# A feed-forward whose first product is made of seven block products instead of eight, on one Trainium2 core

## The chip, the cores and the metric

The kernel runs on one core of one Trainium2 chip. The metric is the device time of one execution in microseconds; three runs of the kernel before are shown, and their median counts.

## What is computed

One layer of a sequence encoder on 512 tokens of width 2048, all in float32. Four mixers (HGRN2, S5, stick-breaking attention, RWKV-7) give `mix`; the part that the change touches is what follows:

```python
mod = c_act @ ada_w[l] + ada_b[l]
shift1, scale1, gate1, shift2, scale2, gate2 = [m[:, None, :] for m in jnp.split(mod, 6, axis=-1)]
...
mix = jnp.concatenate([o_a, o_b, o_c, o_d], axis=-1) @ w_out[l]
x = _layer_norm(DEEPNORM_ALPHA * x + gate1 * mix, ln1_g[l], ln1_b[l])

h = x * (1.0 + scale2) + shift2
ffn = (jax.nn.silu(h @ ffn_w1[l]) * (h @ ffn_w3[l])) @ ffn_w2[l]
x = _layer_norm(DEEPNORM_ALPHA * x + gate2 * ffn, ln2_g[l], ln2_b[l])
```

`ffn_w1` and `ffn_w3` are 2048 x 5632, `ffn_w2` is 5632 x 2048.

## The kernel before

**Products.** Every large product is made in three passes: each operand is split into a high part (ACT rounds it to fp32r) and a low part (DVE subtracts the high part from the value), and `mm3` (L586) multiplies high by high, low by high and high by low, three matmuls into the same PSUM bank. A matmul has a stationary block of 128 x 128 and 512 moving columns. `wload` (L574) brings 256 KB of weights by a DMA on SP's queue into `wr`, casts them to `wh` on ACT and makes `wl` on DVE, with three buffers of each.

**Order.** A scheduler puts the instructions of each engine into one fixed order, by priorities: `tc.high_priority` in `wload` moves a load and its split ahead. Each engine then works through its row, and waits where an operand isn't there yet. Pools of rotating tiles decide how far ahead a load may go: a tile is free again when its last reader is done. PSUM has eight banks, four in the pool `pd` and four in `pm`.

**End of the first half.** `w_out` (L1414) makes the mixers' output product in groups of feature tiles; per column block n four PSUM sums are multiplied by the gate `g1` into `go` and added to `acc` by DVE (`add_out`, L1409). The steps W1, B1 and W2 are the last in `ORDER`. The group 8 to 11 comes after them: its weights are multiplied by the gate beforehand (`wr`), split into `woh` and `wol`, the features into `cath` and `catl`, and the sums go straight into `acc`, t by t, each t with its `layer_norm` (L1195) and a scaling.

**Feed-forward.** 64 transposes on PE turn `acc` into 16 feature tiles (`hf`, then `hh`, `hl`), 128 features x 512 tokens. `ff_pair(f)` (L1503) makes 128 hidden columns: 16 `mm3` for `ffn_w1` into `pu`, 16 for `ffn_w3` into `pv`, with the weights stationary and the features moving; then silu, a product, and a split into `gh`, `gl`. After each eight f (the last time four) comes the second product over them: for four column blocks of 512, four PSUM sums over eight f, gated and added into `acc`. The last group of four has gated weights made beforehand, so that only an addition, a layer norm and eight scalings per t stand behind the last matmuls. The gate `gate2` (part 5 of the modulation) comes from 64 loads `aw` and 64 DVE steps `acc<-aw,cact,acc` that `pump` (L1148) puts between the steps of W1, W2 and `ff_pair`.

Of the kernel before, what the change touches and what calls it, by code (L numbers as in the profile page):

```python
# [573 lines left out]
def wload(E, src, r0, c0, kk, cols):  # L574

    with E.tc.high_priority(offset=E.ahead):
        raw = E.wp.tile([128, kk, cols], F32, name=E.nm("wr"), tag="wr")
        E.nc.sync.dma_start(out=raw, in_=src[r0 : r0 + 128 * kk, c0 : c0 + cols].rearrange("(k p) c -> p k c", p=128))
# [7 lines left out]
def mm3(E, out, a, b, first, last):  # L586

    E.mm(out, a[0], b[0], first, False)
    E.mm(out, a[1], b[0], False, False)
    E.mm(out, a[0], b[1], False, last)  # L590

# [624 lines left out]
def body(ctx, tc, i, out):  # L1216
# [263 lines left out]
    E.h = []  # L1480
    for k in range(KT):
# [5 lines left out]
        hi, lo = E.sb("hh", dt=F32R, pool=E.hp), E.sb("hl", dt=F32R, pool=E.hp)  # L1487
        nc.vector.tensor_copy(out=hi, in_=f)
        E.sub(lo, f, hi.bitcast(F32))
        E.h.append((hi, lo))  # L1490
    ada_queue(E, [(5, b) for b in range(4)])
    E.rate = 1

    for n in range(4):
        w = slice(T * n, T * n + T)
        g, b = bcast(E, i["ln1_g"][0:1, w], "lg"), bcast(E, i["ln1_b"][0:1, w], "lb")
        E.ts(g, g, ALPHA, ALU.mult)
        E.ts(b, b, ALPHA, ALU.mult)
        for t in range(4):
            E.mul(acc[t][n], acc[t][n], g)  # L1500
            E.add(acc[t][n], acc[t][n], b)

    def ff_pair(f):  # L1503
        pu = E.psd()
        for kg in range(4):
            wh, wl = wload(E, i["ffn_w1"][0], T * kg, 128 * f, 4, 128)
            for k in range(4):
                kk = 4 * kg + k
                mm3(E, pu, (wh[:, k], wl[:, k]), E.h[kk], kk == 0, kk == 15)
        pv = E.psd()  # L1510
        for kg in range(4):
            wh, wl = wload(E, i["ffn_w3"][0], T * kg, 128 * f, 4, 128)
            for k in range(4):
                kk = 4 * kg + k
                mm3(E, pv, (wh[:, k], wl[:, k]), E.h[kk], kk == 0, kk == 15)
            pump(E, 5)
        s = E.sb("s")
        E.act(s, pu, AF.Silu)
        E.mul(s, s, pv)
        hi = E.sb("gh", dt=F32R, pool=E.pp)  # L1520
        lo = E.sb("gl", dt=F32R)
        E.copy(hi, s)
        E.sub(lo, s, hi.bitcast(F32))
# [2 lines left out]
    f = 0
    for cnt in (8, 8, 8, 8, 8, 4):
        fs = list(range(f, f + cnt))
        f += cnt
        ws = []  # L1530

        def gated(n, k):
            if k == fs[0]:
                ws.append(bcast(E, E.gate[5][0:1, T * n : T * n + T], "g2", E.ap))
            r = E.sb("wr", pool=E.pp)
            nc.sync.dma_start(out=r, in_=i["ffn_w2"][0, 128 * k : 128 * k + 128, T * n : T * n + T])
            E.mul(r, r, ws[n])
            return r

        if cnt < 8:  # L1540
            raw = {(n, k): gated(n, k) for n in range(3) for k in fs}
        gs = [ff_pair(a) for a in fs]
        if cnt == 8:
            for n in range(4):
                g2 = bcast(E, E.gate[5][0:1, T * n : T * n + T], "g2")
                pss = [E.psm() for _ in range(4)]
                for kk, k in enumerate(fs):
                    wh, wl = wload(E, i["ffn_w2"][0], 128 * k, T * n, 1, T)
                    for t in range(4):
                        w = slice(128 * t, 128 * t + 128)  # L1550
                        mm3(E, pss[t], (gs[kk][0][:, w], gs[kk][1][:, w]), (wh[:, 0], wl[:, 0]), kk == 0, kk == 7)
                for t in range(4):
                    add_out(pss[t], g2, acc[t][n])
        else:
            raw.update({(3, k): gated(3, k) for k in fs})
            ws = {a: E.split(r, "w2", E.hp) for a, r in raw.items()}
            lg = [bcast(E, i["ln2_g"][0:1, T * n : T * n + T], "lg") for n in range(4)]
            lb = [bcast(E, i["ln2_b"][0:1, T * n : T * n + T], "lb") for n in range(4)]
            for t in range(4):
                w = slice(128 * t, 128 * t + 128)  # L1560
                for n in range(4):
                    ps = E.psm()
                    for kk, k in enumerate(fs):
                        mm3(E, ps, (gs[kk][0][:, w], gs[kk][1][:, w]), ws[n, k], kk == 0, kk == cnt - 1)
                    E.add(acc[t][n], acc[t][n], ps)
                mu, rs = layer_norm(E, acc[t])
                for n in range(4):
                    E.stt(acc[t][n], acc[t][n], mu, lg[n], ALU.subtract, ALU.mult)
                    E.stt(acc[t][n], acc[t][n], rs, lb[n], ALU.mult, ALU.add)
                    nc.sync.dma_start(out=out[0, w, T * n : T * n + T], in_=acc[t][n])  # L1570


# [24 lines left out]
```

## Time and profile before

| | us |
|---|---|
| runs | 2560.27, 2562.38, 2572.34 |
| median | 2562.38 |
| profiled execution | 2564.39 |
| its span | 2562.7 |
| granted TensorE clock, mean over the span | 0.992 |

The profile shows one execution. PE is TensorE's matmuls, PEld its weight loads, DVE VectorE, ACT ScalarE, POOL GpSimd, SP the engine that issues most DMAs. A group of instructions is told as line, engine, operation, output and inputs by the program's names, shape and count; then busy time, mean duration in ns of one, and the idle time of the engine ahead of them with what ended it. The duration of a matmul is longer than the distance from one to the next, since they overlap; so what a matmul costs is read from counts over a stretch. The chain that ended last follows the work back from the last instruction.

The stages that matter here, by their times in the profiled execution: the last group of w_out from 1048 us to 1092, the feed-forward from 1099 to 2548, of which the first product is 4224 matmuls and the second 2112, and the end of the last layer norm to 2562.7.

### The profile page before, as it was taken

The numbers are of one execution on the slowest core, as the hardware profiler recorded it, in microseconds if no ns is written. First come the engines' busy times: TensorE is split into PE (matmuls) and PEld (weight loads), VectorE is DVE, ScalarE is ACT, GpSimd is POOL, SyncE is SP. The second block draws the span as 40 slices with busy tenths as digits, with TensorE's granted clock in tenths as the row PEclk, the third lists the DMA queues.
The fourth block names the chain that finished last, engine by engine and source line by source line (L and its number), as shares of the span: only waits on it lengthen the run. The fifth ranks groups of instructions, "written<-read, shape, count | busy, mean of one in ns | idle before, by whom it ended". The sixth has DMA issues, their size and how long they took to land.

```text
span 2562.7 us, 33154 instructions
## 1 busy us (share of the span) xinstructions
PE 2506.0 (98%) x12242; PEld 1966.0 (77%) x12242; DVE 1419.9 (55%) x2562; ACT 801.3 (31%) x1409; POOL 71.5 (3%) x193
## 2 busy tenths in 40 slices
PE   8999999999999989999999999999999999999997
PEld 3557767776788767877888888888888888888886
DVE  3755997466788978895344334433443334334538
ACT  2435242322544643132222222222222222222231
POOL 3300000110000000000000000000000000000000
PEclk9999999999999999999999999999999999999999
DMA  9876235445744676135333333333333333334333
GB/s 296 263 245 189 78 88 141 116 122 157 222 117 127 191 231 209 58 91 181 101 110 99 98 98 108 100 98 97 109 100 98 98 104 105 97 98 141 122 95 109
DMA packets 405874, 340.00 MB, mean 133 GB/s; under 512 B 38374, under 2 KB 325312, under 8 KB 405712
## 3 DMA queue, kind: packets, MB, share of 16 engines
q1 hardware_dynamic: 402976, 337.16, 43.2%
q8 instruction: 96, 1.57, 0.3%
q10 hardware_dynamic: 2256, 0.67, 0.1%
q14 instruction: 66, 0.54, 0.1%
q0 software_dynamic: 480, 0.05, 0.0%
HBM read 330.96 MB, written 6.83 MB: 132 GB/s over the span
## 4 chain that ended last, share of the span: by engine, by line
PE 85%; DVE 7%; DMA 5%; issue 1%; ACT 1%; SPq 0%; DVEq 0%; POOL 0%
PE pd L87 55%; PE pm L87 29%; DMA aw<-in_ada_w_dram 5%; DVE acc L117 2%; DVE wl L99 1%; PE pm L90 1%; DMA wr<-in_w_out_dram 0%; DVE acc L99 0%; DVE st L1200 0%; DVE sl L120 0%; DVE wr L99 0%; SPq L1086 0%; DVE sz L99 0%; ACT wh L96 0%; DVE sl L117 0%
## 5 line engine op out<-in xcount | busy, mean ns | idle before, releaser
L99 DVE TENSOR_TENSOR wl<-wr,wh 128x512 fp32r<-128x512 f32 x748 | 516.5, 692 | 844.3 <-ACT wh L96 791.2
L96 ACT CAST wh<-wr 128x512 fp32r<-128x512 f32 x748 | 463.8, 620 | 1356.2 <-PE pd L87 929.7
L87 PE MATMUL pd<-hh,wl 128*128 128x512 f32 x1920 | 754.6, 393 | 3.6 <-DVE wl L99 3.5
L87 PE MATMUL pd<-hh,wh 128*128 128x512 f32 x1920 | 754.7, 393 | 2.4 <-ACT hh L96 2.4
L87 PE MATMUL pd<-hl,wh 128*128 128x512 f32 x1920 | 753.5, 393 | 0.0
L87 PEld LDWEIGHTS pd<-hh,wh 128*128 128x128 f32 x1920 | 361.6, 188 | 92.2 <-ACT wh L96 8.0
L87 PEld LDWEIGHTS pd<-hh,wl 128*128 128x128 f32 x1920 | 361.6, 188 | 89.9 <-issue 8.7
L87 PEld LDWEIGHTS pd<-hl,wh 128*128 128x128 f32 x1920 | 361.6, 188 | 78.6 <-issue 4.0
L87 PE MATMUL pm<-wl,gh 128*128 128x512 f32 x640 | 249.2, 389 | 0.0
L87 PE MATMUL pm<-wh,gl 128*128 128x512 f32 x640 | 249.1, 389 | 0.0
L87 PE MATMUL pm<-wh,gh 128*128 128x512 f32 x640 | 248.2, 392 | 0.0
L117 DVE SCALAR_TENSOR_TENSOR acc<-aw,cact,acc 128x512 f32<-128x512 f32 x240 | 179.9, 749 | 65.1 <-DMA aw<-in_ada_w_dram 63.2
L87 PEld LDWEIGHTS pm<-wh,gh 128*128 128x128 f32 x640 | 120.1, 188 | 28.6 <-DVE go L99 3.8
L87 PEld LDWEIGHTS pm<-wl,gh 128*128 128x128 f32 x640 | 120.1, 188 | 25.2
L87 PEld LDWEIGHTS pm<-wh,gl 128*128 128x128 f32 x640 | 120.2, 188 | 24.3
L87 PE MATMUL pd<-wh,cath 128*128 128x512 f32 x192 | 76.6, 403 | 7.0 <-DVE go L99 7.0
L87 PE MATMUL pd<-wl,cath 128*128 128x512 f32 x192 | 76.0, 398 | 1.4 <-DVE wl L99 1.4
L87 PE MATMUL pd<-wh,catl 128*128 128x512 f32 x192 | 76.3, 397 | 0.0
L87 PE MATMUL pm<-aw,crep 128*32 128x512 f32 x256 | 71.3, 614 | 4.9 <-DVE hgm L233 4.3
L99 DVE TENSOR_TENSOR acc<-acc,go 128x512 f32<-128x512 f32 x112 | 72.3, 687 | 0.0
L99 DVE TENSOR_TENSOR s<-s,pd 128x512 f32<-128x512 f32 x44 | 30.3, 688 | 55.7 <-PE pd L87 55.7
L99 DVE TENSOR_TENSOR go<-pm,g 128x512 f32<-128x512 f32 x80 | 51.3, 684 | 0.0
(449 smaller groups left out, 2415.5 us busy)
## 6 DMA issues: line engine op xcount, KB each, us to landing
wr<-in_ffn_w_dram SPq DMA_DIRECT2D x528, 256.0 KB, 2.9
aw<-in_ada_w_dram SPq DMA_DIRECT2D x384, 256.0 KB, 3.5
wr<-in_w_in_dram SPq DMA_DIRECT2D x184, 256.0 KB, 3.0
wr<-in_w_out_dram SPq DMA_DIRECT2D x64, 256.0 KB, 3.5
g<-gate SPq DMA_DIRECT2D x36, 256.0 KB, 3.7
x<-in_x_dram SPq DMA_DIRECT2D x16, 256.0 KB, 5.0
acc<-in_x_dram SPq DMA_DIRECT2D x16, 256.0 KB, 5.0
out_dram<-acc SPq DMA_DIRECT2D x16, 256.0 KB, 2.1
```

The costliest lines, as they stand in the source:

```text
L87: return self.nc.tensor.matmul(out=out, lhsT=lhsT, rhs=rhs, start=start, stop=stop, **kw)
L90: self.nc.tensor.transpose(out=out, in_=in_, identity=self.ident)
L96: self.nc.scalar.copy(out=out, in_=in_)
L99: self.nc.vector.tensor_tensor(out=out, in0=a, in1=b, op=op)
L117: self.nc.vector.scalar_tensor_tensor(out=out, in0=a, scalar=s, in1=b, op0=op0, op1=op1)
```

## The change

**First product.** The features and the two weight matrices are seen as blocks. A pair (j, j+8) of feature tiles, each halved into 256 tokens, gives four blocks of the left operand; `ffn_w1` and `ffn_w3`, rows j and j+8, 512 columns, give four blocks of the right one, which is the products' moving operand now. Sums of blocks (Winograd's form of Strassen's scheme) need seven block products where eight were made. Sums of features are made once, before the feed-forward; sums of weights for every j of every block of 512 columns. A block of columns n (eleven of them) has two stages: stage 1 makes p1, p3, p2 over j = 0 to 7 from three quarter-blocks of weights that are only split; stage 2 makes the rest of p1 and p4, p7, p5 from four quarter-blocks, with three sums on DVE (`wx`) and two splits. Then u, v, g1, g2 are put together from the PSUM sums on ACT and DVE, and `turned` transposes the result on PE, splits it and stores it to a DRAM tile `gd`.

**Second product.** It runs after all columns of the first, in two halves r of 1024 output columns; 22 pairs of f each, sums staying in eight PSUM banks over all 44 f. The gated features are read back from `gd`. The sums of `gate2` are made in the first half, four loads and steps in each of 16 pairs. `acc`, normalised, is stored to DRAM (`xn`) ahead of the feed-forward and read back in the second half. The last pair is done t by t, each t followed by gate, sum, layer norm, eight scalings and the stores.

**Pools.** The pools of the first half are opened in stacks that are closed before the feed-forward, and the pools of the weights (`wp`, `ap`, `a1`) already before the last group of w_out, whose gate broadcasts now take tiles of the pool `tp`.

The diff, cut to what the prediction speaks of:

```diff
+    E.high.close()
+    late = ExitStack()
+    E.ax = E.open(late, "ax", 8, side="right")
     grp = (8, 9, 10, 11)
     ws = {}
     for n in range(4):
-        g1 = bcast(E, E.gate[2][0:1, T * n : T * n + T], "g1", E.ap)
+        g1 = bcast(E, E.gate[2][0:1, T * n : T * n + T], "g1")
...
+    for j in range(8):
+        f, e = feature(j), feature(j + 8)
+        a11, a21, a12, a22 = f[:, 0:H], f[:, H:], e[:, 0:H], e[:, H:]
+        s, r = E.sb("hs"), E.sb("hr")
+        s1, s2, s3, s4 = r[:, 0:H], r[:, H:], s[:, 0:H], s[:, H:]
+        E.add(s1, a21, a22)
+        E.sub(s2, s1, a11)
+        E.sub(s4, a12, s2)
+        E.sub(s3, a11, a21)
+        m = {}
+        one = slot("ha")
+        E.copy(one[:, 0:H], a11)
+        E.sub(one[:, H:], a11, one[:, 0:H].bitcast(F32))
+        m["11"] = one[:, 0:H], one[:, H:]
+        m["12"], m["22"] = halves(e, "hb")
+        m["s3"], m["s4"] = halves(s, "hc")
+        m["s1"], m["s2"] = halves(r, "hd")
+        A.append(m)
...
+    E.fx = E.open(ffn_w, "fx", 2)
+    E.fh = E.open(ffn_w, "fh", 4)
+    E.ft = E.open(ffn_t, "ft", 1)
+    E.f2 = E.open(ffn_t, "f2", 2)
+    E.p2 = E.open(last, "p2", 4, space=PSUM)
...
+    def product(p, a, w, c, first, last, **kw):
+        for b in range(2):
+            v = slice(128 * b, 128 * b + 128)
+            mm3(E, p[:, b], (a[0][:, v], a[1][:, v]), (w[0][:, c], w[1][:, c]), first, last, **kw)
...
+        p1, p2, p3 = bank2("p1"), bank2("p2"), bank2("p3")
+        for j in range(8):
+            with tc.high_priority(offset=E.ahead):
+                x = quad(j, n, (0, 2, 3))
+                wa = parts(x[:, 2:4])
+                hi, lo = two(E.fh, "wh", "wh", F32R), two(E.fh, "wl", "wl", F32R)
+                E.copy(hi[:, 0], x[:, 0])
+                E.sub(lo[:, 0], x[:, 0], hi[:, 0].bitcast(F32))
+            product(p1, A[j]["11"], (hi, lo), 0, j == 0, j == 7)
+            product(p3, A[j]["s4"], wa, 0, j == 0, j == 7)
+            product(p2, A[j]["12"], wa, 1, j == 0, j == 7)
+            if before and j == 3:
+                turned(*before)
+        with soon():
+            u, v, g1 = two(E.ft, "u", "u"), two(E.ft, "v", "v"), two(E.f2, "g1", "g1")
+            E.copy(u, p1)
+            E.copy(v, p3)
+            E.add(g1, u, p2)
+            E.act(g1, g1, AF.Silu)
...
+            with tc.high_priority(offset=E.ahead):
+                x = quad(j, n, (0, 1, 2, 3))
+                E.sub(x[:, 0:2], x[:, 1:3], x[:, 0:2])
+                E.sub(x[:, 2], x[:, 2], x[:, 0])
+                E.sub(x[:, 3], x[:, 2], x[:, 3])
+                wb = parts(x[:, 2:4])
+                wa = parts(x[:, 0:2])
+            product(p1, A[j]["s2"], wb, 0, False, j == 7, skip_group_check=True)
+            product(p4, A[j]["22"], wb, 1, j == 0, j == 7)
+            product(p7, A[j]["s3"], wa, 1, j == 0, j == 7)
+            product(p5, A[j]["s1"], wa, 0, j == 0, j == 7)
+        with soon():
+            u = two(E.ft, "u", "u")
+            E.copy(u, p1)
+            E.add(v, v, p1)
+            E.add(u, u, p7)
+            g2 = two(E.ft, "g2", "g2")
+            E.sub(g2, u, p4)
+            E.act(g2, g2, AF.Silu)
+            E.add(v, v, p5)
+            E.add(u, u, p5)
+            E.mul(g1, g1, v)
+            E.mul(g2, g2, u)
+        before = n, (g1, g2)
...
+                                for n in range(2):
+                                    o = E.sb("go", pool=E.fz)
+                                    E.mul(o, pt[t][:, n], g2[2 + n])
+                                    E.add(acc[t][2 + n], acc[t][2 + n], o)
+                                mu, rs = layer_norm(E, acc[t])
```

`parts` casts 1024 columns on ACT (`wh`) and subtracts on DVE (`wl`); `quad` issues one DMA of 256 KB for each quarter-block into `wx`. A `product` is six matmuls of 128x512 into a tile of two banks; `p2` has four such tiles. `halves` splits a 512-column pair of blocks in the same way. Stage 1 has 18 matmuls per j, stage 2 has 24.

How the change moves instructions, in the order of each engine. On DVE, where w_out's last group begins, the row before (`go_2061` and `go_2062` are the last evacuation of W2, `wol` a low part of the gated weights, `acc<-acc,pd` the group's first sums; the weights' gate products `wr<-wr,g1` stand more than 180 rows earlier):

```order
L99 TENSOR_TENSOR acc_1922_8940<-acc_1922_8940,go_2061_9539 128x512
L99 TENSOR_TENSOR acc_1923_8943<-acc_1923_8943,go_2062_9542 128x512
L99 TENSOR_TENSOR wl_2240_10278<-wr_2238_10275,wh_2239_10277 128x512
L99 TENSOR_TENSOR wol_2111_9655<-wr_2109_9651,woh_2110_9654 128x512
L99 TENSOR_TENSOR acc_1809_8412<-acc_1809_8412,pd_2123_9681 128x512
L99 TENSOR_TENSOR wol_2114_9662<-wr_2112_9658,woh_2113_9661 128x512
L99 TENSOR_TENSOR acc_1846_8586<-acc_1846_8586,pd_2124_9695 128x512
```

At the same place in the changed kernel:

```order
L104 TENSOR_TENSOR acc_1922_8940<-acc_1922_8940,go_2061_9539 128x512
L104 TENSOR_TENSOR acc_1923_8943<-acc_1923_8943,go_2062_9542 128x512
L104 TENSOR_TENSOR wr_2064_9553<-wr_2064_9553,g1_2063_9551 128x512
L104 TENSOR_TENSOR wr_2067_9560<-wr_2067_9560,g1_2063_9551 128x512
L104 TENSOR_TENSOR wr_2070_9567<-wr_2070_9567,g1_2063_9551 128x512
L104 TENSOR_TENSOR wol_2066_9557<-wr_2064_9553,woh_2065_9556 128x512
L104 TENSOR_TENSOR wr_2073_9574<-wr_2073_9574,g1_2063_9551 128x512
L104 TENSOR_TENSOR wol_2069_9564<-wr_2067_9560,woh_2068_9563 128x512
```

All 16 gate products, 16 low parts of weights and four of features now stand between W2's last evacuation and the first sum `acc<-acc,pd`, 36 rows in all.

On PE, at the beginning of the feed-forward (`pm<-ident,acc` is a transpose, `hh` and `hl` are features, `wh` and `wl` weights), before:

```order
L90 MATMUL pm_2179_10061<-ident_94,acc_1849_8595 128x128
L87 MATMUL pd_2231_10238<-hh_2161_10013,wh_2233_10241 128x512
L90 MATMUL pm_2183_10072<-ident_94,acc_1846_8586 128x128
L90 MATMUL pm_2183_10072<-ident_94,acc_1847_8589 128x128
L90 MATMUL pm_2183_10072<-ident_94,acc_1848_8592 128x128
L90 MATMUL pm_2183_10072<-ident_94,acc_1849_8595 128x128
L87 MATMUL pd_2231_10238<-hh_2161_10013,wl_2234_10242 128x512
```

In the changed kernel all 64 transposes stand ahead of the first matmul of the feed-forward:

```order
L95 MATMUL pm_2252_10265<-ident_94,acc_1922_8940 128x128
L95 MATMUL pm_2252_10265<-ident_94,acc_1923_8943 128x128
L92 MATMUL p1_2263_10330<-wh_2269_10341,ha_2165_10033 128x512 x2
L92 MATMUL p3_2265_10332<-wh_2267_10337,hch_2168_10040 128x512
L92 MATMUL p1_2263_10330<-wl_2270_10342,ha_2165_10033 128x512
```

The low part `wl_2270` that its third row reads stands in DVE's row behind the last low part of the features' sums, and so do all low parts of weights.

On DVE in the first product, before (`acc<-aw,cact,acc` is a step of the modulation, `s<-s,pd` the product behind the silu):

```order
L99 TENSOR_TENSOR wl_2427_11071<-wr_2425_11068,wh_2426_11070 128x512
L117 SCALAR_TENSOR_TENSOR acc_2366_10814<-aw_2406_10988,cact_88,acc_2366_10814 128x512
L99 TENSOR_TENSOR wl_2430_11089<-wr_2428_11086,wh_2429_11088 128x512
L117 SCALAR_TENSOR_TENSOR acc_2366_10814<-aw_2407_10991,cact_88,acc_2366_10814 128x512
L117 SCALAR_TENSOR_TENSOR acc_2366_10814<-aw_2408_10994,cact_88,acc_2366_10814 128x512
L99 TENSOR_TENSOR s_2421_11060<-s_2421_11060,pd_2401_10966 128x512
```

In the changed kernel, at the beginning of stage 2 of the second block of columns (`wx` are the sums of weights of j = 0, 1, 2, `g1<-u,p2` the sum that waits for stage 1's last matmul):

```order
L104 TENSOR_TENSOR wx_2409_11197<-wx_2409_11197 128x1024
L104 TENSOR_TENSOR wx_2409_11197<-wx_2409_11197 128x512 x2
L104 TENSOR_TENSOR wx_2414_11237<-wx_2414_11237 128x1024
L104 TENSOR_TENSOR g1_2405_11189<-u_2403_11187,p2_2355_10915 128x1024
L104 TENSOR_TENSOR wl_2411_11206<-wx_2409_11197,wh_2410_11205 128x1024
L104 TENSOR_TENSOR wl_2413_11210<-wx_2409_11197,wh_2412_11209 128x1024
L104 TENSOR_TENSOR wx_2414_11237<-wx_2414_11237 128x512 x2
L104 TENSOR_TENSOR wl_2416_11246<-wx_2414_11237,wh_2415_11245 128x1024
L104 TENSOR_TENSOR wl_2418_11250<-wx_2414_11237,wh_2417_11249 128x1024
L104 TENSOR_TENSOR wx_2419_11277<-wx_2419_11277 128x1024
L104 TENSOR_TENSOR wx_2419_11277<-wx_2419_11277 128x512 x2
```

A low part 512 columns wide, one for each 256 KB, has become three sums and two low parts of 1024 columns for each 1 MB, one j after the other.

More of the change, by code (lines that the diff above doesn't have):

```diff
@@ L583, in wload, with mm3 @@
     return hi, lo
[L586 to L590, printed above, removed]
+def mm3(E, out, a, b, first, last, **kw):
+    E.mm(out, a[0], b[0], first, False, **kw)
+    E.mm(out, a[1], b[0], False, False, **kw)
+    E.mm(out, a[0], b[1], False, last, **kw)
 def rw_setup(E):
@@ L1479, in body, with slot, halves, feature @@
     E.add(sh, sh, E.mod[:, 48:64])
-    E.h = []
-    for k in range(KT):
+    H = 256
+    slots = [E.hp] * 32 + [E.pp] * 16 + [E.ax] * 8
+    A = []
+    def slot(name):
+        return E.sb(name, dt=F32R, pool=slots.pop(0))
+    def halves(src, name):
+        hi, lo = slot(name + "h"), slot(name + "l")
+        E.copy(hi, src)
+        E.sub(lo, src, hi.bitcast(F32))
+        return [(hi[:, c : c + H], lo[:, c : c + H]) for c in (0, H)]
+    def feature(k):
         ps = E.psm()
@@ L1486, in body @@
         E.act(f, ps, AF.Identity, scale=sc[:, k : k + 1], bias=sh[:, k : k + 1])
[L1487 to L1523, printed above, removed]
-        return hi, lo
@@ L1526, in body @@
[L1526 to L1548, printed above, removed]
-                    for t in range(4):
[L1550 to L1570, printed above, removed]
@@ new lines, in feature @@
+        return f
+    for j in range(8):
[16 more added lines that the diff above has]
+        A.append(m)
@@ new lines, in body @@
+    for t in range(4):
+        for n in range(4):
+            nc.sync.dma_start(out=xn[t, n], in_=acc[t][n])
+    E.low.close()
+    E.psum.close()
+    ffn_w, ffn_t, last = ExitStack(), ExitStack(), ExitStack()
+    E.fx = E.open(ffn_w, "fx", 2)
[3 more added lines that the diff above has]
+    E.p2 = E.open(last, "p2", 4, space=PSUM)
+    two = lambda p, name, tag, dt=F32: p.tile([128, 2, T], dt, name=E.nm(name), tag=tag)
+    bank2 = lambda name: E.p2.tile([128, 2, T], F32, name=E.nm(name), tag="p")
@@ new lines, in body, with gate_steps @@
+    turned(*before)
+    ffn_t.close()
+    E.sp = E.open(last, "sp2", 12)
+    E.fz = E.open(last, "fz", 18)
+    E.ap_tile = lambda name: E.sb(name, pool=E.fz)
+    sums = [None] * 4
+    def gate_steps():
+        for b in range(4):
+            c0 = 5 * D + T * b
+            a = sums[b] = E.sb("acc", pool=E.fz)
+            for k in range(KT):
+                raw = E.sb("aw", pool=E.fz)
+                nc.sync.dma_start(out=raw, in_=E.ada[:, k, c0 : c0 + T])
+                if k == 0:
+                    E.ts(a, raw, E.cact[:, 0:1], ALU.mult)
+                else:
+                    E.stt(a, raw, E.cact[:, k : k + 1], a, ALU.mult, ALU.add)
+                yield
@@ new lines, in gate_rows @@
+    def gate_rows():
+        ps = bank2("gr")
+        for b in range(4):
+            E.mm(ps[32 * b : 32 * b + 32, 0], E.ones[:, 0:32], sums[b])
+        bias = E.sb("bias", pool=E.fz)
+        for b in range(4):
+            nc.sync.dma_start(out=bias[32 * b : 32 * b + 32], in_=i["ada_b"][0:1, 5 * D + T * b : 5 * D + T * b + T]
+                              .rearrange("o n -> (o n)").partition_broadcast(32))
+        E.add(bias, bias, ps[:, 0])
+        for b in range(4):
+            nc.sync.dma_start(out=E.gate[5][0:1, T * b : T * b + T], in_=bias[32 * b : 32 * b + 1])
+        return [bcast(E, E.gate[5][0:1, T * n : T * n + T], "g2", "fz") for n in range(4)]
@@ new lines, in base, with pair_w2 @@
+    def base(t, n):
+        a = acc[t][n] = E.sb("acc", pool=E.pp)
+        nc.sync.dma_start(out=a, in_=xn[t, n])
+        E.mul(a, a, lg[n])
+        E.add(a, a, lb[n])
+    gs = gate_steps()
+    lg, lb = [None] * 4, [None] * 4
+    y0 = []
+    def pair_w2(f, r):
+        with tc.high_priority(offset=E.ahead):
+            x = E.fx.tile([128, 2, 2, T], F32, name=E.nm("wx"), tag="wx")
+            nc.sync.dma_start(out=x, in_=i["ffn_w2"][0, 128 * f : 128 * f + 256, 1024 * r : 1024 * r + 1024]
+                              .rearrange("(f p) (n t) -> p f n t", p=128, t=T))
+            gg = []
+            for q in range(2):
+                hi, lo = E.sb("gh", dt=F32R, pool=E.hp), E.sb("gl", dt=F32R, pool=E.hp)
+                for s, t in enumerate((hi, lo)):
+                    nc.sync.dma_start(out=t.bitcast(F32), in_=gd[f + q, s])
+                gg.append((hi, lo))
+            return gg, [parts(x[:, q]) for q in range(2)]
@@ L1574 @@
+    last.close()
+    ffn_w.close()
+    late.close()
 _INS = ["x", "c", "ada_w", "ada_b", "w_in", "w_out", "hg_lb_logits", "hg_norm_g", "s5_a_re", "s5_a_im", "s5_log_dt",
```

108 lines of the change are left out of this document (99 added, 9 removed).

## The prediction

> **What bounds the kernel now.** I read the page first: busy time, then the chain that ended last.
>
> ```profile
> span 2562.7 us, 33154 instructions
> PE 2506.0 (98%) x12242; PEld 1966.0 (77%) x12242; DVE 1419.9 (55%) x2562; ACT 801.3 (31%) x1409; POOL 71.5 (3%) x193
> PE 85%; DVE 7%; DMA 5%; issue 1%; ACT 1%; SPq 0%; DVEq 0%; POOL 0%
> ```
>
> PE is busy in 98% of the span and carries 85% of the chain, so a matmul left out of the feed-forward is worth its pitch. The pitch comes from a table by stretches (columns: stretch, length, then busy time with instruction count for PE, weight loads, DVE, ACT, POOL, then granted clock, DMA share, GB/s).
>
> ```profile
> 1048.40:1091.70 43.30, 43.30 (x192) 35.86 (x191) 36.16 (x84) 1.13 (x2) 0.00 (x0) 1.00 0.08 24
> 1096.00:1098.00 2.00, 1.18 (x5) 0.79 (x6) 2.00 (x5) 0.92 (x2) 0.00 (x0) 0.66 0.00 0
> 1098.00:1100.00 2.00, 2.00 (x9) 1.93 (x10) 1.93 (x4) 2.00 (x4) 0.00 (x0) 0.50 0.00 0
> 1300.00:1400.00 100.00, 100.00 (x441) 82.24 (x441) 45.73 (x71) 24.14 (x39) 0.00 (x0) 1.00 0.33 105
> 2548.00:2562.00 14.00, 0.35 (x2) 0.00 (x0) 11.08 (x26) 0.00 (x0) 0.00 (x0) 0.60 0.40 150
> ```
>
> In the feed-forward 441 matmuls take 100 us: 0.2267 us each, with DVE 46% and ACT 24% busy and PE never waiting. The last product of w_out (first row) runs its 192 matmuls at that pitch, 43.3 us. After 2548 PE is done and the span is a tail of DVE work, 14.5 us to the end at 2562.7.
>
> Next, how long DVE and ACT take for the shapes that the change uses, and how they hand over. By form, and from the timeline (start, length):
>
> ```profile
> L99 DVE TENSOR_TENSOR wl<-wr,wh 128x512 fp32r<-128x512 f32 x748 | 516.5, 692 | 844.3 <-ACT wh L96 791.2 <-PE pm L87 40.2 <-PE pd L87 4.1
> L99 DVE TENSOR_TENSOR hx<-hx,hq 128x256 f32<-128x256 f32 x28 | 11.9, 424 | 1.1 <-ACT hx L93 1.1
> L96 ACT CAST wh<-wr 128x512 fp32r<-128x512 f32 x748 | 463.8, 620 | 1356.2 <-PE pd L87 929.7 <-PE pm L87 351.7 <-issue 26.8
> L93 ACT ACTIVATE hx<-hd 128x256 f32<-128x256 f32 x56 | 20.5, 414 | 16.8 <-DVE hd L99 16.6
> 1046.93 1.28 DVE L99 TENSOR_TENSOR go<-pd,g 128x512 f32<-128x512 f32 x2
> 1048.12 1.28 DVE L99 TENSOR_TENSOR acc<-acc,go 128x512 f32<-128x512 f32 x2
> 1049.33 1.28 DVE L99 TENSOR_TENSOR go<-pd,g 128x512 f32<-128x512 f32 x2
> 1286.46 0.62 ACT L96 CAST wh<-wr 128x512 fp32r<-128x512 f32 x1 [1.19 <-PE pm L87]
> 1287.11 0.69 DVE L99 TENSOR_TENSOR wl<-wr,wh 128x512 fp32r<-128x512 f32 x1 [1.11 <-ACT wh L96]
> ```
>
> DVE: 692 ns at 512 columns and 424 at 256, so 1.047 ns a column and, drawn on, 1.23 us at 1024. One that doesn't read its predecessor starts 0.60 after it (two 0.69 ops in 1.28), so 1024 columns start 1.14 apart, 256 columns 0.33. ACT likewise: 620 and 414 ns, 1.03 us at 1024. A hand-over from ACT to DVE costs 0.03 (1286.46 + 0.62 to 1287.11).
>
> **The change part by part.** *Matmuls.* The order of the changed kernel has 336 feed-forward matmuls for each of eleven column blocks, 3696 for 4224. 528 × 0.2267 = **−119.7 us**. The second product keeps its 2112.
>
> *Stage 2 of each column block.* For each j DVE now runs five operations in a fixed order: three sums (1024, 512, 512 columns, each next reading the one before), then the two low parts (1024 each). The first low part waits for ACT's cast, which waits for the third sum. Per j: 1.26 + 0.72 + 0.69 (sums, dependent starts) + 0.04 + 1.04 + 0.03 (cast with its hand-overs) + 1.14 + 1.14 = 6.06 us. PE needs 24 × 0.2267 = 5.44. So DVE, idle or not, sets the pace. The rotating buffers let it be one j ahead at the start, and there it also stands behind the sum g1, which waits for stage 1's last matmul: g1 ends 1.3 us into the stage, j = 0's low parts at 3.6, the two sums left of j = 1 at 5.0, as if j = 1 had begun at 2.33 (5.0 less the sums' 2.67). Six more j make 38.7, and PE can start on j = 7 with its cast, 3.75 later: 42.5. The stage ends at 42.5 + 5.44 = 47.95 for 8 × 5.44 = 43.5: +4.4 in ten blocks, +2 in the first (g1 stands better there), **+46**. Bounds: 0 (were S at or below 5.44) and +60 (if each DVE operation began only when the one before had ended: 2 × 0.09 more in S, 7 × 0.18 in each of eleven blocks, +14).
>
> *Start of stage 1 and the turning.* After stage 2 DVE has the last low parts, then seven 1024-wide sums and products of the evacuation, 8.0 us, and the low parts of j = 1 stand behind six of them. PE has 16 matmuls and two transposes to do before; 1.4 to 2.8 us are left, 2.1 taken: × 10 = **+21** (0 to +33, with the four stores a block that stand in SP's queue ahead of the next loads). The turning adds 16 transposes a block, 176 in all.
>
> ```profile
> 1095.98 0.56 DVE acc L114
> 1096.54 0.04 issue
> 1096.59 0.47 PE pm L90
> ...
> 1100.26 0.44 PE pm L90 x4
> ...
> 1106.49 177.39 PE pd L87 x767
> ```
>
> Four take 0.44 us on the chain, so 176 × 0.109 = **+19.2**. Their casts, low parts and stores go beside stage 1, where DVE has 1.14 + 0.60 of 4.08 us per j to do.
>
> *The last product of w_out.* Before, its gated weights were made long ahead among DVE's waits; two low parts were left when it began. Now the pool of the broadcasts and the stacks put all 36 operations (16 gate products, 16 low parts, 4 of the features) into DVE's order behind the last evacuation of W2, and ahead of the first sum of results. Say W2 ends at E (1048.4 before). The evacuation took 1046.93 to 1051.7, so it ends at E + 3.3; 36 × 0.60 = 21.6 more: E + 24.9. PE reaches the row that reads the last feature's low part there, does its remaining 30 rows of the first t (6.8), 144 rows (32.6) and pays a cold clock of 1.5 us: E + 66, for 43.4 before: **+22.6** (+19 to +26, 36 × 0.69). The clock is from the rows above: after PE's 3.2 us without work to 1096.59 it was granted 0.66, then 0.50 for 2 us (0.34 × 1.4 + 0.50 × 2 lost). DVE had these 36 in W1 and W2 before, where PE sometimes waits for it:
>
> ```profile
> PE pd L87 <- DVE go L99: 7.0, 5, 2.3
> PE pd L87 <- DVE wl L99: 1.6, 3, 0.7
> ```
>
> Of these waits (860 to 1010 us) I take **−8** back (0 to −14).
>
> *The operands.* Before, the layer norm's end, 64 transposes and the feature casts lay between 1091.7 and 1106.5 with PE already in the feed-forward; 1106.49 + 177.39 us for 767 matmuls puts an undisturbed start at about 1108.4, E + 60. Now each j takes eight DVE operations, five of 256 columns and three of 512: 5 × 0.33 + 3 × 0.60 = 3.45, and 0.3 for the ones that read their predecessor or wait for a cast: 3.75 us. Eight make 30 us, all ahead of the first low part of a weight in DVE's order, so PE waits for all. E + 66 + 6.2 (layer norm's end) + 7 (first features) + 30, less 2 of high-part work: E + 107, so 41 behind the product where it was 16.5: **+24.4** (+18 to +32).
>
> *Between the products and in the second.* DVE's 8 us of evacuation hold the PSUM that the second product needs: 5 us, plus 1.5 of cold clock, **+6.5** (+3 to +13). In the second product a pair of f has 48 × 0.2267 = 10.9 us on PE and 2 × 1.14 + 4 × 0.66 = 4.9 on DVE (0.66 is a scaling's start to start, below), so DVE hides; **+5.5** at the ends of the halves, where PSUM is emptied. The modulation's 64 loads, moved here from beside the first product, 1 MB in each pair of the first half, stand in SP's queue with 1 MB of weights and 1 MB of stored features: nine issues of 0.33 us, and 3.15 MB in 10.9 us, 289 GB/s.
>
> ```profile
> 5.00:15.00 10.00, 9.59 (x30) 2.40 (x29) 0.29 (x1) 0.00 (x0) 9.12 (x35) 1.00 1.02 317
> 25.00:35.00 10.00, 10.00 (x32) 5.54 (x30) 3.60 (x7) 1.59 (x3) 3.04 (x15) 0.84 1.01 320
> wr<-in_ffn_w_dram SPq DMA_DIRECT2D x528, 256.0 KB, 2.9
> 1287.83 0.33 SPq L578 DMA_DIRECT2D wr<-in_ffn_w_dram  x1
> ```
>
> The full queues gave 317 and 320, so it fits with little to spare. In stage 2 a j loads 1 MB in 6 us, 173 GB/s; four issues and a landing of 2.9 us are done in 4.5, under 6.06.
>
> *The tail.* The last pair of rows is done t by t, so the first t is complete 3 × 12 matmuls (8.2 us) before PE ends at P, and DVE's row of work from there is 16 products and sums, 14 statistics, 4 merges, 32 scalings and 40 small ones.
>
> ```profile
> 2547.27 0.69 DVE L1200 BATCH_NORM_STATS2 st<-acc 128x6 f32<-128x512 f32 x1
> 2548.05 1.42 DVE L117 SCALAR_TENSOR_TENSOR acc<-acc,lnr,lb 128x512 f32<-128x512 f32 x2
> 2545.82 0.15 DVE L117 SCALAR_TENSOR_TENSOR lnr<-lnt,lnr 128x1 f32<-128x1 f32 x1
> ```
>
> 16 × 0.60 + 14 × 0.60 + 4 × 0.27 + 32 × 0.66 + 40 × 0.12 = 45 us: it ends at P + 37, the span 3.3 later, P + 40. Before PE had 10.9 us of matmuls per t beside it and the end came at P + 14.5: **+25.5** (+22 to +30).
>
> Sum: −119.7 + 46 + 21 + 19.2 + 22.6 − 8 + 24.4 + 6.5 + 5.5 + 25.5 = +43.0. The profiled execution took 2564.4 us (span 2562.7), 2.0 above the median of the runs shown, so the forecast is 2562.4 + 43 = **2605 us**.
>
> **The rivals.** *Faster: stage 2 keeps PE's pace.* Its place is the cast inside DVE's five operations. If S is 5.44 or less, the 46 go, and with DVE no longer late at the stage's end also the 21: 2605 − 67 = **2538 us**. It decides at S = 5.44, 0.62 below mine; DVE's own starts sum to only 4.62 and nothing in before shows an operation of 1024 columns. Against it is the order, in which nothing stands between the third sum and the waiting low part.
>
> *Slower: loads become the bound.* If three streams get 250 GB/s instead of 317 (the stretch 940:950 got this beside busy engines, below), a pair takes 3.15/0.25 = 12.6 us for 10.9, in 16 pairs +27: **2632 us**.
>
> ```profile
> 940.00:950.00 10.00, 8.15 (x37) 6.45 (x36) 7.43 (x12) 1.86 (x3) 0.00 (x0) 1.00 0.80 253
> ```
>
> *Slower: short waits cool the clock.* PE now waits about a microsecond at many places. If each block costs one 4 us stretch at 0.50, that is +2 us × 11 = +22: **2627 us**. In 940:950 PE was without work for 1.85 us and the clock stayed at 1.00, which speaks against it. The Trainium skill, "TensorE: Matmul & The Clock Gate", section "A second HAM failure mode: psum-queue depth-cycling", tells of such an oscillation with short idles between groups of matmuls.
>
> *Slower: no overlap on DVE.* If an operation waits for the end of the one before, stage 2 costs the 14 of the bound above and the 36 operations of w_out 36 × 0.09 = 3 more: **2622 us**. The rows speak against it: two operations of 0.69 us are done in 1.28. The Trainium skill, "VectorE: DVE Perf Modes", section "The DRAIN you can't avoid", says that the next operation doesn't start until the pipe is empty.
>
> *No change in the work*, if the products weren't fewer: the order counts 336 a block, so I give it nothing.
>
> **How the numbers follow.** Forecast case 0.56, stage 2 at PE's pace 0.16, loads 0.14, clock 0.10, no overlap 0.04. A measurement here tells 0.5%, 12.8 us, from no change (2549.6 to 2575.2). Of the faster rival 0.11 lies below 2549.6 and 0.05 in the band; of the forecast, with several low bounds together, 0.06 reaches into the band. So faster 0.11, same 0.11, slower 0.78. The range goes from 2555 (15 left of the 67 us of the two pace terms) to 2650 (the forecast with the load term and 18 us of the other high bounds); about 0.13 lies below and 0.07 above.
>
> **What would show it.** In the profile of the changed kernel: windows of 84 us per block with 336 matmuls and PE busy 77.9; low parts of stage 2 released by ACT's cast and PE by DVE's low part; a stretch of about 40 us without matmuls after w_out's last product and 25 before its first rows; 40 us from PE's last matmul to the end. I am wrong if blocks take under 80 us, or if PE in stage 2 waits for DMA, or if the stretch before the feed-forward is under 25 us.

## The result, and the profile after

| | us | to before |
|---|---|---|
| before, median of 4 runs | 2561.32 | |
| changed, median of 4 runs (2634.84 to 2651.49) | 2646.90 | 1.0317, 95% interval 1.0272 to 1.0362 |
| changed, span of the profiled execution | 2643.7 | 2562.7 before |

The changed kernel is 3.2% slower: 2647 us where 2605 was forecast. The page of the profile after:

```profile
span 2643.7 us, 33043 instructions
PE 2470.3 (93%) x11890; PEld 1885.3 (71%) x11890; DVE 1738.4 (66%) x2629; ACT 930.1 (35%) x1350; POOL 71.8 (3%) x193
PE 26%; DVE 16%; DMA 12%; issue 6%; ACT 4%; SPq 2%; DVEq 0%; ACTq 0%
```

The work left out is gone, and PE's busy time fell by only 36 us; the chain that ended last, as far as it can be followed back (66% of the span), is 26% PE, and DVE with 16% and DMA with 12% stand in it. By stretches (busy time with count of PE, weight loads, DVE, ACT, POOL, then granted clock, DMA share, GB/s), the changed kernel's stages in order of time:

```profile
1041.40:1101.60 60.20, 47.77 (x192) 37.89 (x193) 49.81 (x106) 9.99 (x17) 0.00 (x0) 0.84 0.14 53
1101.60:1139.50 37.90, 15.99 (x65) 10.39 (x63) 35.08 (x82) 28.27 (x51) 0.00 (x0) 0.55 0.20 69
1139.60:2114.30 974.70, 916.65 (x3856) 705.05 (x3856) 703.77 (x718) 387.42 (x426) 0.00 (x0) 0.98 0.59 195
1490.90:1528.00 37.10, 35.28 (x161) 28.36 (x159) 23.82 (x25) 15.89 (x19) 0.00 (x0) 1.00 0.67 227
1528.20:1579.70 51.50, 47.93 (x193) 36.09 (x194) 41.14 (x42) 19.47 (x20) 0.00 (x0) 0.97 0.50 162
2114.30:2121.80 7.50, 1.00 (x6) 0.82 (x5) 7.50 (x7) 4.45 (x5) 0.00 (x0) 0.82 0.58 217
2121.80:2605.10 483.30, 483.30 (x2134) 399.22 (x2132) 195.73 (x233) 94.90 (x95) 0.00 (x0) 1.00 0.66 229
2605.10:2643.70 38.60, 0.17 (x1) 0.00 (x0) 35.15 (x88) 0.00 (x0) 0.00 (x0) 0.53 0.29 109
```

These are w_out's last product (W2 ended at 1034.9), the operands, the whole first product, one stage 1 and one stage 2 of it, the stretch between the products, the second product and the tail. Each set beside the same part of the kernel before:

| part | before | after | measured | forecast |
|---|---|---|---|---|
| W2's end | 1048.4 | 1034.9 | −13.5 | −8 |
| from there to the end of w_out's product | 43.3 | 66.7 | +23.4 | +22.6 |
| operands, to the feed-forward's start | 16.7 | 38.0 | +21.3 | +24.4 |
| first product | 957.6 | 974.7 | **+17.1** | **−33.5** |
| between the products | 0 | 7.4 | +7.4 | +6.5 |
| second product | 478.8 | 483.3 | +4.5 | +5.5 |
| PE's waits in the feed-forward before | 3.4 | | −3.4 | 0 |
| PE's last matmul to the end | 14.5 | 38.6 | +24.1 | +25.5 |
| sum of the spans | | | +80.9 | +43.0 |

Before, the first product is 4224 and the second 2112 matmuls of 0.2267 us, and the 3.4 are what is left up to 2548.2. Every part came within 6 us of its forecast but one: the first product is longer than the one it replaces. A block of columns takes 88.6 us (974.7 by 11), where 84.0 was worked out (924.1 by 11) and PE alone needs 77.9.

Why a block is long shows in DVE's row and in SP's. DVE in the middle of stage 2 (start, length):

```profile
1545.42 2.67 DVE L104 TENSOR_TENSOR wx<-wx 128x1024 f32<-128x1024 f32 x3
1549.28 2.36 DVE L104 TENSOR_TENSOR wl<-wx,wh 128x1024 fp32r<-128x1024 f32 x2 [1.19 <-ACT wh L101]
1551.56 2.67 DVE L104 TENSOR_TENSOR wx<-wx 128x1024 f32<-128x1024 f32 x3
```

One j takes 6.14 us (1545.42 to 1551.56), with 1.19 of waiting for the cast: the forecast's 6.06. At the start of the same stage, the chain:

```profile
1523.40 0.33 SPq L1558
...
1524.25 5.10 DMA wx<-in_ffn_w_dram
...
1529.47 0.06 DVE wx L104
1529.53 1.08 issue
1530.62 0.15 DVE g L104
1530.77 0.98 issue
1531.74 2.35 DVE wl L104 x2
```

PE begins the stage at 1528.2. The load for j = 1 is issued from 1523.40 on, since SP waits until DVE has freed one of the two tiles; it lands at 1529.35. The first sum of j = 1 waits for it, g1 stands behind that sum and ends at 1531.8, 3.6 us into the stage where 1.3 was worked out, and j = 0's low parts stand behind g1. What PE then does:

```profile
1528.20:1532.00 3.80, 2.04 (x7) 1.08 (x8) 2.53 (x3) 1.93 (x3) 0.00 (x0) 1.00 0.35 134
1532.00:1536.00 4.00, 3.98 (x10) 2.71 (x11) 3.39 (x4) 1.41 (x2) 0.00 (x0) 0.57 0.22 52
```

It stands for 1.8 us, and then runs 4 us at a granted clock of 0.57. Within 21 us it has made this up, and waits again for the cast of every j, as here:

```profile
1549.30 0.50 PE L92 MATMUL p<-wh,hdh 128*128 128x512 f32 x1 [0.31 <-ACT wh L101]
```

Four more such waits follow, one for each j left, about 6.14 us apart, which is DVE's pace: DVE's row, begun late, sets the end of the stage.

### The profile page after: what moved, and what is told of

Same layout as the page of the kernel before. It is cut to its first block, busy times and chain, and to the rows that moved or that the text cites. A ratio compares the mean times of both kernels' runs of the same rounds, so it can differ in the third digit from the quotient of the medians.

```text
span 2643.7 us, 33043 instructions
## 1 busy us (share of the span) xinstructions
PE 2470.3 (93%) x11890; PEld 1885.3 (71%) x11890; DVE 1738.4 (66%) x2629; ACT 930.1 (35%) x1350; POOL 71.8 (3%) x193
## 4 chain that ended last, share of the span: by engine, by line
PE 26%; DVE 16%; DMA 12%; issue 6%; ACT 4%; SPq 2%; DVEq 0%; ACTq 0%
PE pt L92 18%; DMA wx<-in_ffn_w_dram 12%; PE pd L92 6%; DVE wl L104 6%; DVE wx L104 5%; ACT wh L101 3%; SPq L1558 2%; PE p L92 1%; DVE g L104 1%; DVE v L104 1%; DVE acc L122 0%; DVE y L122 0%; DVE wr L104 0%; DVE st L1205 0%; DVE wol L104 0%
## 5 line engine op out<-in xcount | busy, mean ns | idle before, releaser
L104 DVE TENSOR_TENSOR wl<-wx,wh 128x1024 fp32r<-128x1024 f32 (+1 forms) x440 | 475.1, 1115 | 387.2 <-ACT wh L101 385.3
L101 ACT CAST wh<-wx 128x1024 fp32r<-128x1024 f32 (+1 forms) x440 | 409.0, 965 | 877.9 <-PE pt L92 332.2
L92 PE MATMUL pt<-wh,gh 128*128 128x512 f32 x704 | 274.7, 390 | 0.0
L92 PE MATMUL pt<-wl,gh 128*128 128x512 f32 x704 | 274.4, 390 | 0.0
L92 PE MATMUL pt<-wh,gl 128*128 128x512 f32 x704 | 274.3, 390 | 0.0
L101 ACT CAST wh<-wr 128x512 fp32r<-128x512 f32 x236 | 145.8, 620 | 339.1 <-PE pd L92 233.2
L104 DVE TENSOR_TENSOR wx<-wx 128x512 f32<-128x512 f32 (+1 forms) x264 | 229.2, 868 | 42.9 <-DMA wx<-in_ffn_w_dram 37.2
L104 DVE TENSOR_TENSOR wl<-wr,wh 128x512 fp32r<-128x512 f32 x236 | 162.3, 691 | 127.6 <-ACT wh L101 106.1
L92 PE MATMUL pd<-hh,wl 128*128 128x512 f32 x512 | 206.6, 403 | 3.5 <-DVE wl L104 3.3
L92 PE MATMUL pd<-hh,wh 128*128 128x512 f32 x512 | 206.1, 404 | 2.4 <-ACT hh L101 2.4
L92 PE MATMUL pd<-hl,wh 128*128 128x512 f32 x512 | 205.1, 401 | 0.0
L92 PE MATMUL p<-wh,hdh 128*128 128x512 f32 x352 | 149.7, 425 | 31.9 <-ACT wh L101 22.6
```

The source lines that it names most:

```text
L92: return self.nc.tensor.matmul(out=out, lhsT=lhsT, rhs=rhs, start=start, stop=stop, **kw)
L101: self.nc.scalar.copy(out=out, in_=in_)
L104: self.nc.vector.tensor_tensor(out=out, in0=a, in1=b, op=op)
```

## The experiments

**A third tile for the loads.** The question was whether the late loads or DVE's chain of sums, cast and low parts makes the blocks long.

```diff
-    E.fx = E.open(ffn_w, "fx", 2)
+    E.fx = E.open(ffn_w, "fx", 3)
...
-            hi, lo = two(E.f2, "gh", "gh", F32R), two(E.f2, "gl", "gl", F32R)
+            hi, lo = two(E.ft, "gh", "gh", F32R), two(E.ft, "gl", "gl", F32R)
...
-    E.fz = E.open(last, "fz", 18)
+    E.fz = E.open(last, "fz", 14)
```

> The changed kernel with three tiles for the loaded weights instead of two (room for it: the turned features' tiles are single, and the second product's pool has 14 tiles for 18). Theory A (loads wait for their tile): with two tiles a load is issued only when DVE's low part has freed one; four issues (1.8 us) and a landing of 4.1 to 4.4 us make stage 1 turn round in 9.3 us for two j, 4.6 a j for the 4.08 that PE needs, and at the start of stage 2 the sums of j = 1 come 2.3 us late, and g1 behind them. Then stage 1 falls from 37.3 to about 35, stage 2 from 51.3 to about 48.5 (DVE's 6.14 us a j stay): 5 us a block, 45 to 60 us in all, time near 2595. Theory B (only DVE's chain of sums, cast and low parts sets the pace): no change within 10 us.

Measured: 2564.37 us, 1.0007 to before (0.9988 to 1.0026), 82 us less than the changed kernel. The whole first product, and a stage 2 and a stage 1:

```profile
1139.90:2033.30 893.40, 873.68 (x3856) 714.98 (x3856) 702.07 (x722) 405.34 (x429) 0.00 (x0) 0.99 0.65 213
1499.90:1543.80 43.90, 43.84 (x192) 36.15 (x193) 35.92 (x38) 19.12 (x20) 0.00 (x0) 1.00 0.59 195
1543.90:1578.50 34.60, 34.60 (x161) 28.37 (x159) 25.65 (x28) 15.68 (x18) 0.00 (x0) 1.00 0.68 222
```

More than either theory had: stage 2 went to PE's own 43.9 us, so DVE's 6.14 us a j did not stay. DVE's row shows why:

```profile
1591.28 1.22 DVE L104 TENSOR_TENSOR wx<-wx 128x1024 f32<-128x1024 f32 x1
1592.42 1.22 DVE L104 TENSOR_TENSOR wl<-wx,wh 128x1024 fp32r<-128x1024 f32 x1
1593.55 1.41 DVE L104 TENSOR_TENSOR wx<-wx 128x512 f32<-128x512 f32 x2
1594.88 1.22 DVE L104 TENSOR_TENSOR wl<-wx,wh 128x1024 fp32r<-128x1024 f32 x1
1596.02 1.22 DVE L104 TENSOR_TENSOR wx<-wx 128x1024 f32<-128x1024 f32 x1
```

The sums of the next j stand between a j's two low parts and fill the wait for the cast: 1591.28 to 1596.02, 4.74 us a j. With a third tile the scheduler had another j's weights to order in. So the edit changed two things, the loads' lead and DVE's order. Beside the two stretches shown, a block has a wait of PE ahead of stage 2, for ACT's copy `u` out of PSUM: 1.5 to 2.7 us ahead of nine of the eleven.

**The third tile with DVE's order held.** To part the two, the first sum of each j takes a factor 1.0 made from the last low part of the j before:

```diff
-                E.sub(x[:, 0:2], x[:, 1:3], x[:, 0:2])
+                one = E.cp.tile([128, 1], F32, name=E.nm("one"), tag="one")
+                E.ts(one, wa[1][:, 1, T - 1 : T].bitcast(F32), 0.0, ALU.mult, 1.0, ALU.add)
+                E.stt(x[:, 0:2], x[:, 1:3], one, x[:, 0:2], ALU.mult, ALU.subtract)
```

> Three tiles for the loads, but DVE's order of the changed kernel in stage 2: the first sum of each j takes a factor 1.0 from one column that a small operation makes out of the last low part of the j before, so no sum can stand ahead of it. The third tile alone gained 82 us, more than theory A gave it, and its order shows the next j's sums between a j's two low parts. Theory C (the third tile works through both: the loads come in time, and the sums of the next j fill the wait for the cast): stage 1 stays at 34.65 us (loads in time), stage 2 goes back to 48.5 to 50.5 us (6.14 us a j, 0.2 more for the small operation), first product near 935 us for 893 with three tiles and 975 with two, time near 2605. Theory A alone (loads are all): stage 2 stays near 44.5, time near 2567. Theory B alone (the wait for the cast is all): both stages as in the changed kernel, time near 2650.

Measured: 2610.74 us, 1.0189 (1.0161 to 1.0216). The first product, a stage 1, a stage 2, and DVE at the start and in the middle of that stage 2:

```profile
1137.20:2081.90 944.70, 891.26 (x3856) 697.57 (x3856) 731.86 (x808) 393.30 (x429) 0.00 (x0) 1.00 0.61 203
1393.30:1428.70 35.40, 34.78 (x161) 28.30 (x159) 25.88 (x28) 16.18 (x19) 0.00 (x0) 1.00 0.75 249
1428.90:1479.20 50.30, 46.10 (x192) 35.05 (x193) 41.06 (x48) 19.30 (x20) 0.00 (x0) 1.00 0.48 157
```

```profile
1427.01 2.36 DVE L104 TENSOR_TENSOR wl<-wx,wh 128x1024 fp32r<-128x1024 f32 x2 [1.19 <-ACT wh L101]
...
1429.59 1.28 DVE L122 SCALAR_TENSOR_TENSOR wx<-wx,one 128x1024 f32<-128x1024 f32 x1
1430.79 1.21 DVE L104 TENSOR_TENSOR g<-u,p 128x1024 f32<-128x1024 f32 x1
...
1443.60 1.28 DVE L122 SCALAR_TENSOR_TENSOR wx<-wx,one 128x1024 f32<-128x1024 f32 x1
...
1450.12 1.28 DVE L122 SCALAR_TENSOR_TENSOR wx<-wx,one 128x1024 f32<-128x1024 f32 x1
```

Theory C: with the order held, stage 1 goes from 37.1 to 35.4 and the first product from 974.7 to 944.7; the free order does the rest, to 893.4. In stage 1 the gain is the loads', since DVE's order there is the changed kernel's. At the start of a stage 2 the order is not held: the added factor puts j = 0's low parts (1427.01) ahead of j = 1's first sum (1429.59) and g1 (1430.79), where the changed kernel has them behind both, so a late load of j = 1 would no longer stand in their way. What loads and order each gain there, this run does not part.

A j takes 6.52 us here, 0.38 more than in the changed kernel by the added operation, and seven of those in eleven blocks are 29 us. Without it the third tile and the new start of stage 2 would have gained about 60 us, and the free order about 20. That split is worked out, not measured.

**The cast under the sums, with two tiles.** Order alone, loads as in the changed kernel:

```diff
                 E.sub(x[:, 0:2], x[:, 1:3], x[:, 0:2])
+                E.copy(wa[0], x[:, 0:2])
                 E.sub(x[:, 2], x[:, 2], x[:, 0])
                 E.sub(x[:, 3], x[:, 2], x[:, 3])
-                wb = parts(x[:, 2:4])
-                wa = parts(x[:, 0:2])
+                E.copy(wb[0], x[:, 2:4])
+                E.sub(wa[1], x[:, 0:2], wa[0].bitcast(F32))
+                E.sub(wb[1], x[:, 2:4], wb[0].bitcast(F32))
+            product(p7, A[j]["s3"], wa, 1, j == 0, j == 7)
+            product(p5, A[j]["s1"], wa, 0, j == 0, j == 7)
             product(p1, A[j]["s2"], wb, 0, False, j == 7, skip_group_check=True)
             product(p4, A[j]["22"], wb, 1, j == 0, j == 7)
-            product(p7, A[j]["s3"], wa, 1, j == 0, j == 7)
-            product(p5, A[j]["s1"], wa, 0, j == 0, j == 7)
```

> The changed kernel with stage 2 written so that ACT casts the first pair of sums while DVE makes the other two, and the products that use the first pair first. Theory B: DVE no longer waits for a cast, a j takes 1.26 + 0.72 + 0.69 + 1.14 + 1.14 = 4.95 us for 6.14, under PE's 5.44, so stage 2 falls from 51.3 to 44 to 46: 55 to 75 us in all, time near 2580. Theory A: the two tiles of loads then hold it: end of j to sums of j + 2 is 6.1 us of load, so two j take 4.95 + 6.1 = 11.05, 5.5 a j, and the late start stays: stage 2 near 48, 30 to 40 us in all. If neither the cast nor the loads matter: no change.

Measured: 2605.97 us, 1.0148 (1.0115 to 1.0180), 41 us less than the changed kernel. Its first product, a stage 1, a stage 2, and what PE waits for in the whole first product (us in total, times, longest):

```profile
1148.90:2078.90 930.00, 887.80 (x3856) 715.70 (x3856) 705.67 (x719) 395.00 (x426) 0.00 (x0) 0.98 0.62 204
1570.80:1608.00 37.20, 37.20 (x160) 30.50 (x161) 24.10 (x25) 15.44 (x19) 0.00 (x0) 0.93 0.64 214
1608.00:1653.30 45.30, 44.33 (x193) 35.70 (x191) 38.54 (x39) 18.74 (x19) 0.00 (x0) 1.00 0.59 188
```

```profile
PE p L92 <- DVE v L104: 28.0, 10, 3.5
```

Stage 2 did what theory B said (45.3 us), yet the time is theory A's: 2.8 us a block came back as a new wait at the start of stage 1, where PE needs the PSUM that v's sum frees. Ahead of the stage 1 shown, PE's last matmul of stage 2 starts at 1566.82, and v's sum stands in DVE's row behind a low part of the next stage 1 that waits for its cast:

```profile
1568.35 1.23 DVE L104 TENSOR_TENSOR wl<-wx,wh 128x1024 fp32r<-128x1024 f32 x1 [4.22 <-ACT wh L101]
1569.49 1.21 DVE L104 TENSOR_TENSOR v<-v,p 128x1024 f32<-128x1024 f32 x1
```

The products now end with p1 and p4, which frees this PSUM later too; but with both edits (below) they end in the same way, and the ten waits come to 9.6 us for 28.0, so that is not the whole cause. Behind this wait the clock falls, 0.93 over the stage 1 shown, which has PE busy throughout and yet takes 37.2 us for the 34.8 that it takes at full clock (below).

**Both edits together.**

> Both edits together. If A and B each hold a part, stage 2 goes to 44 to 45 us (43.5 is PE alone) and stage 1 to 35: a block of 79 to 80 for 88.6, 95 to 105 us in all, time near 2545. If the clock (granted 0.98 in the blocks) is a cause of its own, 1.5 us a block stay.

Measured: 2556.41 us, 0.9962 (0.9943 to 0.9982). The first product takes 885.8 us at a clock of 1.00; below it a stage 1:

```profile
1139.10:2024.90 885.80, 869.10 (x3856) 708.83 (x3856) 695.63 (x721) 403.59 (x429) 0.00 (x0) 1.00 0.65 214
1461.60:1496.40 34.80, 34.80 (x160) 28.72 (x161) 26.94 (x29) 17.75 (x20) 0.00 (x0) 1.00 0.68 223
```

Stages of about 34.8 and 44 to 45 us with 1 between make 80 to 81 a block; the expectation's 79 to 80 was near, and the time is 11 us over its 2545. Only 8 us more than with the third tile alone, since that had already hidden the cast.

**The gate broadcasts back in their old pool.**

```diff
-    E.high.close()
-    late = ExitStack()
-    E.ax = E.open(late, "ax", 8, side="right")
...
-        g1 = bcast(E, E.gate[2][0:1, T * n : T * n + T], "g1")
+        g1 = E.ap.tile([128, T], F32, name=E.nm("g1"), tag="aw")
+        nc.sync.dma_start(out=g1, in_=E.gate[2][0:1, T * n : T * n + T].rearrange("o n -> (o n)").partition_broadcast(128))
...
     cs = [E.split(cat[k], "cat", E.pp) for k in grp]
+    E.high.close()
+    late = ExitStack()
+    E.ax = E.open(late, "ax", 8, side="right")
```

> The changed kernel with the four gate broadcasts of w_out's last group in the pool that they had before, closed only behind them. Theory: the 36 DVE operations that now stand behind W2 stand there because the broadcasts take tiles that come free late; back in their old pool they are made in W1 and W2, PE's product begins at once behind W2 and takes 43.4 us again for 66.7: 23 us gained, of which up to 6 go back to W1 and W2 (W2 ended 13.5 us earlier than before), time near 2628. Rival: the closing of the stacks (which tiles wait for which) sets it, and nothing changes.

Measured: 2622.74 us, 1.0211 (1.0181 to 1.0241), by the medians 24 us less than the changed kernel and by the spans of the profiled executions 14 (2629.7). W_out's last product, behind a W2 that ends at 1042.7:

```profile
1042.90:1086.50 43.60, 43.60 (x194) 36.04 (x194) 35.26 (x82) 0.62 (x1) 0.00 (x0) 1.00 0.20 73
```

It takes 43.6 us again, 23 less, and W2 ends 7.8 later than in the changed kernel, when DVE has the 36 operations in W1 and W2 again. So the change of pool, with the closing that goes with it, put them behind W2. The old pool is one of those that are closed, so the edit moves both, and the two are not parted.

**Together, and the tail.** `best1` has the three edits. `best_tail` also makes the last two pairs of the second product t by t:

```diff
+            if r == 1 and f == NFT - 4:
+                held = gg, ww
-            if f == 0 or f == NFT - 2:
+            elif f == 0 or f == NFT - 2:
                 for t in range(4):
                     if f == 0:
                         pt[t] = bank2("pt")
+                    if r == 1 and f:
+                        for q in range(2):
+                            mm_w2(pt[t], t, q, *held, f - 2)
```

> Three tiles, the stage 2 with the cast under the sums, and the gate broadcasts of w_out's last group in their old pool, together. If the gains of fx3hide (90 us from the changed kernel) and of gate (24 us) stand in different stages they add: 2647 - 114 = 2533, 1.1% under the kernel before. If W2's end moves with the pools (it ended 8 us later in gate), 2541.

> The same with the last two pairs of rows of the second product done t by t, so that the first t is complete 3 x 24 matmuls (16.3 us) before PE's end and not 8.2. Theory (DVE's 45 us of work for the four t's, begun when the first is complete, sets the end): 8 us less from PE's last matmul to the end (38.6 in the changed kernel), less what PE waits for the second pair's low parts (0 to 3 us): 5 to 8 us under best1. Rival (the end hangs on the last t's chain alone): no change.

Measured: 2538.67 us, 0.9899 (0.9879 to 0.9918), and 2531.16 us, 0.9873 (0.9851 to 0.9894), both as expected. The tail of `best1` takes 38.6 us, as in the changed kernel (2497.7 to 2536.3); that of `best_tail`:

```profile
2497.70:2529.40 31.70, 0.19 (x1) 0.00 (x0) 28.03 (x71) 0.00 (x0) 0.00 (x0) 0.58 0.27 100
```

PE's last matmul ends at 2497.7 in both, and the tail is 6.9 us shorter: DVE's row of work from the first complete t sets the end.

## Why the prediction was right in sign and 42 us short

**Right.** Slower, and by the places named: w_out's last group (23.4 for 22.6, and `gate` shows its cause), the operands (21.3 for 24.4), the stretch between the products, the second product, the tail (24.1 for 25.5, and `best_tail` shows its cause). DVE's j in stage 2 took 6.14 us for 6.06, and `hide` shows that the cast inside it matters. PE's waits in the first product end with ACT's cast (50.1 us in 85 waits, 11.4 of them before its first matmul) more than with DVE's low part (9.0 in 16), which the prediction had named.

**Luck.** The time lies 3 us under the top of the range, 2650, which was reached with a load term for the second product and parts of other high bounds. In the second product nothing of that term was found, so that the range held is in part luck. None of the three signs of being wrong came up either: PE itself never waits for a DMA in stage 2; DVE and ACT wait in its place.

**The step that failed** is the sentence on loads: "four issues and a landing of 2.9 us are done in 4.5, under 6.06", costed at nothing. Two things are wrong in it. The landing is 4.1 us in the median of the first product's loads, issued three or four at a time, not the 2.9 of the kernel before, which issues one at a time:

```profile
wx<-in_ffn_w_dram SPq DMA_DIRECT2D x616, 256.0 KB, 4.1
```

And the comparison was made with stage 2's period alone. In stage 1 a j takes PE 4.08 us, and two tiles, each taken again only when DVE has freed it, can't turn round that fast; and the load for stage 2's j = 1 must come in stage 1's last period. In the first product of the changed kernel (engine, waits for, us in total, times, longest):

```profile
ACT wh L101 <- DMA wx<-in_ffn_w_dram: 169.6, 71, 8.0
DVE wx L104 <- DMA wx<-in_ffn_w_dram: 37.2, 31, 2.9
```

ACT's casts of stage 1, which read the loads as they are, and DVE's sums of stage 2 stand behind the loads. With the third tile ACT's waits fall to 53.8 us (31 times; in `fx3seq` 49.3, 24 times). DVE's rise to 60.6, since DVE is ahead there, so such a row shows a loss only together with the stage's length. By the starts of PE's matmuls the ten stages 2 behind the first take 51.2 us in the mean, for the 47.95 worked out, and the ten stages 1 37.9 for 36.5 (32.6 of matmuls, 1.7 of transposes, 2.1 of waiting): 32 and 14 of the 50 us by which the first product missed. The third tile shortens stage 1 in `fx3seq` without help from the order; at the start of stage 2 that run does not part the two.

**The rivals.** "Loads become the bound" named the right resource in the wrong place: in the second product, where it was priced, PE was busy for all of the 483.3 us at 229 GB/s. "Short waits cool the clock" had a tenth of the chance and a price of 22 us. The clock did fall, near the start of nine of the eleven stages 2, and over the first product it is 0.98, about 19 us of 974.7. But this is not what the product lost, since PE makes it up before DVE's row ends the stage. Two stages 2 of the changed kernel part the two causes:

```profile
1795.50:1847.10 51.60, 46.75 (x193) 34.89 (x194) 41.04 (x42) 19.41 (x20) 0.00 (x0) 1.00 0.51 166
1884.90:1933.80 48.90, 47.05 (x192) 36.57 (x193) 39.86 (x42) 19.25 (x20) 0.00 (x0) 0.97 0.49 161
```

In the first DVE waits 2.71 us for j = 1's load and the clock stays at 1.00; in the second the clock falls, and j = 1's load does not keep DVE waiting. Of the ten stages 2 behind the first, the two without a fall take 50.5 and 51.6 us, the eight with one 48.9 to 52.1. The long stages go with the late load, not with the fall of the clock: most of the miss in stage 2 is the late load's. It adds to the pace terms, which the forecast treated as a case apart.

"Stage 2 at PE's pace" needed an order that the changed kernel didn't have; with the third tile it had it. From the forecast's 924.1 us for the first product the third tile comes to 893.4 and both edits to 885.8: 31 and 38 of the 67 us that this rival was given. "No overlap on DVE" is out: two low parts of 1.22 us took 2.36.

## What to carry to other kernels

Work out a load's turn-round (free, issue, land, use) for every stage with its own period, not for the longest one, and count tiles by it; a tile more also lets the scheduler order the next step's work into this step's waits. Fewer matmuls pay only where the engine that prepares their operands has time left in that stage: here 12.5% fewer cost three DVE operations more for each 1 MB of weights in stage 2, and the saving came out only when loads, order and pools were set for it. Count one-time work on both sides of a loop (operands, pool closings, what stands behind the last matmul) at full length; here w_out's group, the operands, the stretch between the products and the tail came to 76 us.
